# A three-branch block and two hybrid layers on one core: HGRN-2 traced among RWKV-7's steps, x normalized before the products, the gates last

## The chip, the cores and the metric

The kernel runs on one core of one Trainium2 chip. The metric is device microseconds (us) of a whole execution. Three runs of the kernel before gave 3648.86, 3641.06 and 3642.4 us, a median of 3642.4 us. Engines are named as in the profile: PE is TensorE (PEld its weight loads), DVE VectorE, ACT ScalarE, POOL GpSimd, SP SyncE, which here only starts transfers.

## The reference, cut to what matters

512 tokens of 1024 features pass through a first block and then two hybrid layers (the change touches only the first block and how its neighbours are traced). The first block in float32:

```
xn = rmsnorm(x, norm1_w);  p = xn @ w_in            # z, xbc, dt | rwkv | hgrn | gates
y_ssm  = ssd_branch(z, xbc, dt)   @ w_branch_ssm    # state space, chunks of 128 tokens
y_rwkv = rwkv7_branch(p_rwkv)     @ w_branch_rwkv   # 8 heads of 64, both directions
y_hgrn = hgrn2_branch(p_hgrn)     @ w_branch_hgrn   # 4 heads of 128, both directions
gates  = sigmoid(p_gate)                            # 3 x 1024 columns
x = x + (g0 * y_ssm + g1 * y_rwkv + g2 * y_hgrn) @ w_out
x = x + ffn(rmsnorm(x, norm2_w))

# RWKV-7, per head and direction:
S_t = S_{t-1} diag(w_t) + (S_{t-1} (-kk_t)) (kk_t * a_t)^T + v_t k_t^T ;  y_t = S_t r_t
# HGRN-2, per head and direction:
S_t = diag(f_t) S_{t-1} + k_t v_t^T ;  o_t = S_t^T q_t
```

## The kernel before, in words

Activations lie with features on the partitions, 512 tokens along the free axis, split into two float16 parts (`xh`, `xl`). Weights come from DRAM in units of 512 KB (eight 128 x 128 blocks), each split into a high and a low float16 part (`_emit_unit`, ACT and DVE, in the first block every second background unit ACT and POOL, line 1055). A product of 128 output features is 8 blocks x 3 matmuls of 512 columns (`fm_g`, lines 1169 to 1171); a product by token (`tm`) is 96 matmuls of 128 columns. I call the first kind a wide product, of 24 wide matmuls.

A scheduler orders the instructions of each engine. Work traced as foreground keeps its order roughly; work traced as background (`bgmode`), after it, is moved into the gaps. Foreground wide products in the first block all go to one PSUM bank (`acc=1`), background ones to two other banks (`bg`). Each kind has a weight stream of its own, in the order of the tables FOREGROUND and BACKGROUND.

The first block runs so. `start()` loads x, splits x times the gain into parts, sums squares, and leaves 1/rms as a row `rb` (line 1297), by which every product is multiplied when it leaves PSUM (`conv_pad` line 247, HGRN line 801, gates line 1310). Then `rwkv()` goes through four tiles of two heads. For each tile `rwkv_mid` builds the causal products `G` of the 8 chunks x 2 heads x 2 directions and inverts I + A: the 32 x 32 diagonal blocks go out to DRAM (`pd`, line 432) and come back as `M` with one block's rows per partition (line 441); DVE solves for X in two interleaved chains of small operations (lines 463 and 466); X goes out to DRAM (line 470) and back into `G` (line 473); the blocks above the diagonal come from small matmuls (lines 480 to 491). `rwkv_scan` then steps through 8 chunks with both directions side by side, and inside it `rwkv_in` prepares the next tile. I call the part of a tile from the first exchange to the scan the inverse.

HGRN-2 (`hgrn`, four heads; per head three wide products and two by token, then seven levels of masked score products, lines 840 to 848) and 16 of the 24 gate tiles are traced after `rwkv` as background. SSD comes next as foreground, with background of its own: the up projections of the RWKV and HGRN outputs (`wbr`, `wbh`), the last 8 gate tiles, and the up projection of SSD's output (`wbs`). The up projections sum into `mg` (line 1333); the output projection `wo1` and the feed-forward follow, then the two hybrid layers.

Of the kernel before, what the change touches and what calls it, by code (L numbers as in the profile page):

```python
# [12 lines left out]
BF16 = mybir.dt.bfloat16  # L13
AF = mybir.ActivationFunctionType
# [5 lines left out]
T = 512  # L20
# [12 lines left out]
def blocks(*ws):  # L33
    """[K, N] matrices with N a multiple of 128 -> units of 8 blocks of 128 x 128, each
    unit with its rows on the partitions; the blocks run over columns, then rows."""
    seq = []
    for w in ws:
        k, n = w.shape
        seq.append(w.reshape(k // 128, 128, n // 128, 128).transpose(2, 0, 1, 3).reshape(-1, 128, 128))
    b = np.concatenate(seq) if len(seq) > 1 else seq[0]  # L40
    return np.ascontiguousarray(b.reshape(-1, UB, 128, 128).transpose(0, 2, 1, 3))


def paired(a, b):
    """Blocks of two matrices, a column tile of each in turn."""
# [25 lines left out]
def gate_up(a, name, *ws):  # L71
    """The column tiles FF7 for products in sevens, the others for plain ones."""
# [5 lines left out]
def odd_even(w):  # L78
    """The odd and the even column tiles."""
# [5 lines left out]
#: Column tiles of the second block's w_in (without the 16 mLSTM gates) in the order of use.  # L85
# [9 lines left out]
#: The same for the first block's (without the 32 steps of the state space branch).  # L95
# [8 lines left out]
def first_constants():  # L104
    """Selectors of heads and masks of the chunks' orders."""
# [16 lines left out]
class Packed:  # L122
    """Small vectors side by side in one array; the program finds them by name."""
# [46 lines left out]
def arrange(x):  # L170
    """The kernel's inputs as the program reads them."""
# [55 lines left out]
def run(gen):  # L227
    """A generator's work at once; its result."""
# [6 lines left out]
class First:  # L235
    """The first block's layer: state space (SSD), RWKV-7 and HGRN-2 branches."""
# [4 lines left out]
    def conv_pad(self, ps, side):  # L241
        """psum / rms with zeros on either side."""
# [4 lines left out]
        nc.vector.tensor_tensor(out=xp[:, 2:T + 2], in0=ps, in1=self.rb, op=ALU.mult)  # L247
        return xp

# [1 line left out]
    def shifted(self, it, n, out):  # L251
        """Token shift in both directions of column tile n."""
# [6 lines left out]
    def half_sigmoid(self, out, ps, hb):  # L259
        """0.5 + 0.5 tanh: the sigmoid of (psum / WS + bias), hb half the bias."""  # L260
# [14 lines left out]
    def rwkv(self, yd):  # L275
        """Chunks of 64 tokens, both directions side by side, a tile of two heads after the
        other; the backward direction keeps its keys and values reversed within the chunks."""
# [34 lines left out]
        for j in range(4):  # L312
            self.rwkv_mid(j)
            scan = self.rwkv_scan(j)
            for c in range(8):
                if c == 2 and j < 3:
                    run(self.rwkv_in(j + 1, it, lx))
                if c == 4 and j < 3:
                    self.rwkv_decays(j + 1, lx)
                next(scan)  # L320
            run(scan)
            self.rwkv_out(j, gx, yd)

    def rwkv_in(self, j, it, lx):
        """What a tile of two heads needs of the projections."""
# [7 lines left out]
        yield from self.shifted(it, j, r)  # L333
        ks = self.bank()
# [5 lines left out]
        yield from self.shifted(it, 8 + j, vf)  # L340
        pr = self.bank()
# [54 lines left out]
    def rwkv_mid(self, j):  # L396
        """Keys and queries with their decays, all causal products of a chunk, (I + A)^-1."""
# [17 lines left out]
        # (source: b or k, i) x (target: kk or r, t) for every direction, chunk and head  # L415
# [12 lines left out]
        # the 32 x 32 diagonal blocks of I + A inverted, one block's even or odd rows a partition  # L428
        pd = self.t(self.dram, [2, 32, 32, 32], "pd")
# [1718 lines left out]
```

## Time and profile before

| what | us |
|---|---|
| runs: median (lowest, highest) | 3642.4 (3641.06, 3648.86) |
| profiled execution: its span | 3644.9 |
| start: loads, norm, first products | 0 to 87.4 |
| RWKV-7 with HGRN-2 and gates behind it | 87.4 to 680.0 |
| SSD up to its last matmul | 680.0 to 960.5 |
| rest of the background up to `wo1` | 960.5 to 1034.8 |
| `wo1`, feed-forward, two hybrid layers | 1034.8 to 3644.9 |

The table cuts the span at places that can be found in the trace: 87.4 and the starts of the later tiles (228.2, 380.6, 519.9) are the first causal products of a tile on PE (line 424's), 680.0 the end of the last tile's output, 960.5 the end of SSD's last small matmul (line 767), 1034.8 the first matmul of `wo1`. The profiled execution's span is 0.07% above the median of the runs.

### The profile page before, as it was taken

The numbers are of one execution on the slowest core, as the hardware profiler recorded it, in microseconds if no ns is written. First come the engines' busy times: TensorE is split into PE (matmuls) and PEld (weight loads), VectorE is DVE, ScalarE is ACT, GpSimd is POOL, SyncE is SP. The second block draws the span as 40 slices with busy tenths as digits, with TensorE's granted clock in tenths as the row PEclk, the third lists the DMA queues.
The fourth block names the chain that finished last, engine by engine and source line by source line (L and its number), as shares of the span: only waits on it lengthen the run. The fifth ranks groups of instructions, "written<-read, shape, count | busy, mean of one in ns | idle before, by whom it ended". The sixth has DMA issues, their size and how long they took to land. (4 is left out here: it accounts for less than half of the span.)

```text
span 3644.9 us, 60827 instructions
## 1 busy us (share of the span) xinstructions
PE 3388.2 (93%) x23758; PEld 2045.0 (56%) x23758; DVE 2751.5 (75%) x5599; ACT 1624.4 (45%) x3033; POOL 751.7 (21%) x762
## 2 busy tenths in 40 slices
PE   7899898898899999999989999999999989999998
PEld 3566565554445567655545545568655545545567
DVE  6767867587577798688767677788688767767788
ACT  4232232455444444364456544444364456634344
POOL 1322223223332212101110131211101120132211
PEclk9897999999999999999999999999999999999999
DMA  4211212333352234322323353335322323353233
GB/s 137 70 49 40 64 40 63 131 111 113 106 171 94 97 99 142 108 74 75 106 76 100 106 170 99 98 112 159 106 73 72 105 81 101 108 172 123 94 99 98
DMA packets 151157, 368.17 MB, mean 101 GB/s; under 512 B 44098, under 2 KB 47428, under 8 KB 150868
## 3 DMA queue, kind: packets, MB, share of 16 engines
q1 hardware_dynamic: 117492, 336.03, 29.5%
q0 software_dynamic: 7680, 23.00, 1.9%
q10 hardware_dynamic: 25696, 5.25, 0.8%
q8 instruction: 186, 3.05, 0.3%
q14 instruction: 103, 0.84, 0.1%
HBM read 322.72 MB, written 40.04 MB: 100 GB/s over the span
## 5 line engine op out<-in xcount | busy, mean ns | idle before, releaser
L1169 PE MATMUL acc<-xh,whi 128*128 128x512 f16 x1224 | 469.3, 383 | 33.0 <-DVE w L753 11.8
L1171 PE MATMUL acc<-xh,wlo 128*128 128x512 f16 x1224 | 469.1, 383 | 20.6 <-DVE wlo L1059 20.3
L1170 PE MATMUL acc<-xl,whi 128*128 128x512 f16 x1224 | 469.6, 384 | 0.0
L1058 ACT ACTIVATE whi<-wst 128x1024 f16<-128x1024 f32 x240 | 250.0, 1049 | 263.4 <-PE acc L1170 141.7
L1059 DVE SCALAR_TENSOR_TENSOR wlo<-wst,whi 128x1024 f16<-128x1024 f32 x240 | 319.0, 1329 | 15.4 <-ACT whi L1058 14.9
L1169 PE MATMUL bg<-xh,bhi 128*128 128x512 f16 x788 | 311.1, 395 | 9.9 <-DVE hi L811 8.2
L1171 PE MATMUL bg<-xh,blo 128*128 128x512 f16 x788 | 310.5, 394 | 5.8 <-DVE reset L309 3.2
L1170 PE MATMUL bg<-xl,bhi 128*128 128x512 f16 x788 | 311.1, 395 | 0.0
L1171 PEld LDWEIGHTS <-wlo 128*128 128x128 f16 x1632 | 160.7, 98 | 232.5 <-DVE wlo L1059 46.4
L1170 PEld LDWEIGHTS <-whi 128*128 128x128 f16 x1632 | 160.5, 98 | 213.0 <-issue 41.6
L1169 PEld LDWEIGHTS <-whi 128*128 128x128 f16 x1632 | 161.1, 99 | 193.8 <-ACT whi L1058 13.5
L1428 POOL TENSOR_TENSOR w<-w,w 128x512 f32<-128x512 f32 x66 | 117.0, 1773 | 445.4 <-DVE w L1428 280.1
L1059 DVE SCALAR_TENSOR_TENSOR blo<-bst,bhi 128x1024 f16<-128x1024 f32 (+1 forms) x156 | 180.5, 1162 | 34.4 <-ACT bhi L1058 32.7
L1204 PE MATMUL acc<-whi,xh 128*128 128x128 f16 x1152 | 195.1, 219 | 2.1 <-DVE bias L1843 1.2
L1058 ACT ACTIVATE bhi<-bst 128x1024 f16<-128x1024 f32 (+1 forms) x156 | 136.4, 887 | 133.0 <-PE bg L1170 95.7
L1206 PE MATMUL acc<-whi,xl 128*128 128x128 f16 x1152 | 195.0, 219 | 0.0
L1205 PE MATMUL acc<-wlo,xh 128*128 128x128 f16 x1152 | 195.0, 219 | 0.0
L1171 PEld LDWEIGHTS <-blo 128*128 128x128 f16 x1172 | 117.0, 100 | 131.3 <-issue 16.3
L1170 PEld LDWEIGHTS <-bhi 128*128 128x128 f16 x1172 | 117.1, 100 | 130.7 <-issue 29.0
L1169 PEld LDWEIGHTS <-bhi 128*128 128x128 f16 x1172 | 117.3, 100 | 114.7 <-issue 15.1
L1204 PEld LDWEIGHTS <-xh 128*128 128x128 f16 x1408 | 139.9, 99 | 15.2 <-issue 5.0
L1205 PEld LDWEIGHTS <-xh 128*128 128x128 f16 x1408 | 140.0, 99 | 6.8 <-issue 5.0
(665 smaller groups left out, 9117.2 us busy)
## 6 DMA issues: line engine op xcount, KB each, us to landing
wst<-win SPq DMA_DIRECT2D x92, 512.0 KB, 3.6
bst<-win SPq DMA_DIRECT2D x64, 512.0 KB, 3.7
wst<-wff SPq DMA_DIRECT2D x60, 512.0 KB, 3.6
bst<-w SPq DMA_DIRECT2D x44, 512.0 KB, 3.5
gd<-bw SPq DMA_DIRECT2D x88, 256.0 KB, 2.1
ug<-gd SPq DMA_DIRECT2D x88, 256.0 KB, 2.7
wst<-w SPq DMA_DIRECT2D x34, 512.0 KB, 3.5
wst<-wf SPq DMA_DIRECT2D x30, 512.0 KB, 3.4
```

The source lines that it names most:

```text
L1058: nc.scalar.activation(out=hi[:, h], in_=st[:, h], func=AF.Copy, scale=WS)
L1059: nc.vector.scalar_tensor_tensor(out=lo[:, h], in0=st[:, h], scalar=WS, in1=hi[:, h], op0=ALU.mult, op1=ALU.subtract)
L1169: mm(ps, lhsT=wh, rhs=h[:, k, :], start=(k == 0), stop=False)
L1170: mm(ps, lhsT=wh, rhs=l[:, k, :], start=False, stop=False)
L1171: mm(ps, lhsT=wl, rhs=h[:, k, :], start=False, stop=(k == nk - 1))
L1204: mm(o, lhsT=xh, rhs=wh, start=(k == 0), stop=False)
L1205: mm(o, lhsT=xh, rhs=wl, start=False, stop=False)
L1206: mm(o, lhsT=xl, rhs=wh, start=False, stop=(k == 7))
L1428: tt = lambda eng, o, x, y, op=ALU.add: eng.tensor_tensor(out=o, in0=x, in1=y, op=op)
```

## The change

Five things are changed together; comments and docstrings are also taken out, so line numbers shift by about 15. First, `start()` sums squares first and multiplies x by `rb` before the split, so that products need no factor by token: what multiplied on DVE or POOL becomes an ACT copy or an ACT tanh out of PSUM. Second, HGRN's level mask is a predicated copy in place of a multiplication and an addition. Third, the exchange of the 32 x 32 blocks goes through PE and PSUM in place of DRAM, the solve is one chain, and `M` and `X` are read at a stride of 32 floats. Fourth, the scan's state is added by PE (a product with the identity). Fifth, `hgrn` is a generator that yields after each part, and `beside()` takes 0.62 of a step at each step of `rwkv`; its weights stand in FOREGROUND among RWKV's, its products go to the one foreground bank, and all 24 gate tiles are traced in SSD's background, ahead of the up projections.

```
 conv_pad:
-        nc.vector.tensor_tensor(out=xp[:, 2:T + 2], in0=ps, in1=self.rb, op=ALU.mult)
+        nc.scalar.activation(out=xp[:, 2:T + 2], in_=ps, func=AF.Copy, scale=IWS)
 rwkv:
         for j in range(4):
-            self.rwkv_mid(j)
+            for _ in self.rwkv_mid(j):
+                beside()
...
                 next(scan)
+                beside()
 rwkv_mid, exchange and solve:
-        for q in range(2):
-            s = slice(32 * q, 32 * q + 32)
-            nc.scalar.dma_start(out=pd[q].rearrange("m i t -> i m t"), in_=G[s, :, s])
...
-            (nc.scalar, nc.sync)[q].dma_start(out=M[s], in_=pd.rearrange("q m i t -> (q m) i t"))
...
+        M = self.t(mid, [128, 1024], "M")
+        for u in range(2):
+            ps = self.b("S")
+            for t in range(16):
+                for q in range(2):
+                    s = slice(32 * q, 32 * q + 32)
+                    mm(ps[s, 32 * t:32 * t + 32], lhsT=G[:, :, 32 * q + 16 * u + t], rhs=self.ident[:, s], start=True, stop=True)
+            for h in range(2):
+                nc.scalar.copy(out=M[64 * h:64 * h + 64, 512 * u:512 * u + 512], in_=ps[0:64])
+        Mv = M.rearrange("p (t i) -> p i t", i=32)
...
+        Xv = X[:, 0:1024].rearrange("p (t r) -> p r t", r=32)
...
         for i in range(31):
-            for c, n in rs:    # c: two chains
-                v.tensor_tensor(out=t, in0=X[c][:, 0:n, i:i + 1]..., in1=M[:, i:i + 1, ts]..., op=ALU.mult)
-            for c, n in rs:
-                v.tensor_tensor(out=X[c][:, 0:n, ts], in0=X[c][:, 0:n, ts], in1=t, op=ALU.subtract)
+            v.tensor_tensor(out=t, in0=Xv[:, rs, i:i + 1]..., in1=Mv[:, i:i + 1, ts]..., op=ALU.mult)
+            v.tensor_tensor(out=Xv[:, rs, ts], in0=Xv[:, rs, ts], in1=t, op=ALU.subtract)
+            if i % 6 == 5:
+                yield
-        for q in range(2):
-            for c in range(2):
-                nc.scalar.dma_start(out=pd2[:, :, :, c, q]..., in_=X[c][64 * q:64 * q + 64])
-        for q in range(2):
-            nc.scalar.dma_start(out=G[s, :, s], in_=pd2[q].rearrange("m r c e t -> (r c e) m t"))
+        for k in range(8):
+            for h in range(2):
+                mm(px[:, 64 * k:64 * k + 64], lhsT=X[:, o:o + 128], rhs=self.ident[:, 64 * h:64 * h + 64], start=(h == 0), stop=(h == 1))
...
+                if q:
+                    nc.scalar.copy(out=dst, in_=src)
+                else:
+                    v.tensor_copy(out=dst, in_=src)
+        for i in range(32):
+            mm(pt[i // 16][0:32, ...], lhsT=Xv[:, i // 2 * 2 + 1], rhs=self.ident[...], start=True, stop=True)
 rwkv_scan, the state:
-                    v.tensor_tensor(out=zf, in0=z.rearrange("p d k -> p (d k)"), in1=pz[:, 0:256], op=ALU.add)
-                    v.tensor_tensor(out=four_v(zf), in0=four_v(zf), in1=zb, op=ALU.mult)
+                    if z is not None:
+                        mm(o, lhsT=self.ident, rhs=z[:, d], start=True, stop=False)
...
+                v.tensor_tensor(out=zn..., in0=pz[:, 0:256]..., in1=zb, op=ALU.mult)
 hgrn, the level mask:
-                    v.tensor_tensor(out=t, in0=po..., in1=hm[:, l:l + 1].to_broadcast([128, 4, 128]), op=ALU.mult)
-                    nc.gpsimd.tensor_tensor(out=sc, in0=sc, in1=t, op=ALU.add)
+                    v.copy_predicated(sc, hm[:, l:l + 1].bitcast(U16).to_broadcast([128, 4, 128]), po...)
 first:
+                def beside():
+                    at[0] += 0.62
+                    while at[0] >= 1:
+                        at[0] -= 1
+                        next(hg, None)
-                self.rwkv(yd[0])
+                self.rwkv(yd[0], beside)
...
                     self.background(
+                        self.gates("w1", 14, 24, gd),
                         self.up(gd, 1, "wbr", *yr, 4, True),
                         self.up(gd, 2, "wbh", *yg, 4),
-                        self.gates("w1", 14, 8, gd),
                         self.up(gd, 0, "wbs", *ysm, 8, False, rbs),
 start:
             for k in range(8):
-                self.norm_tile(k, x[:, k], gain)
-            self.norm_end()
+                self.square_sums(k, x[:, k], None, eng=nc.vector)
+            self.norm_end(1.0)
+            for k in range(8):
+                (nc.gpsimd if k % 3 == 1 else nc.vector).tensor_tensor(out=x[:, k], in0=x[:, k], in1=self.rb, op=ALU.mult)
+                self.split(self.xh[:, k, :], self.xl[:, k, :], x[:, k], self.col(gain, k))
 gates, in the first block:
-                nc.scalar.copy(out=g, in_=ps)
-                nc.gpsimd.tensor_tensor(out=g, in0=g, in1=self.rb, op=ALU.mult)
+                nc.scalar.activation(out=g, in_=ps, func=AF.Tanh, scale=0.5 * IWS)
-FOREGROUND = [ ("w1", 0, 14), ("w1", 38, 58), ...
+FOREGROUND = [ ("w1", 0, 5), ("w1", 58, 63), ("w1", 5, 8), ("w1", 63, 68), ...
-    nc = _bacc.Bacc("TRN2", target_bir_lowering=False, num_devices=1)
+    nc = _bacc.Bacc("TRN2", target_bir_lowering=False, num_devices=1, dynamic_dma_scratch_size=4096)
```

How the order of instructions changes is shown at three places. The first is ACT's queue at the end of the first tile's inverse. Before (`bw` is a gate, `hw` HGRN's, `w` the transposed blocks):

```order
L1309 COPY bw_4320<-bg_4287 128x512
L1313 ACTIVATE bw_4320<-bw_4320 128x512
L815 ACTIVATE hw_4087<-hg_3981 128x512
L470 DMA pd_121_712<-X_114_562 512x1x32 x2
L470 DMA pd_121_712<-X_113_561 512x1x32 x2
L473 DMA G_506<-pd_121_712 32x32x32 x2
L482 COPY w_736<-S_719 32x512
```

Now the same place, with HGRN's products (`hk`, `hi`, `hg`) leaving PSUM between the two exchanges:

```order
L445 COPY M_648<-S_649 64x512 x2
L445 COPY M_648<-S_684 64x512 x2
L1074 ACTIVATE whi_818<-wst_816 128x1024
L821 ACTIVATE hk_612<-acc_757 128x512
L826 ACTIVATE hi_815<-acc_822 128x512
L1074 ACTIVATE whi_947<-wst_945 128x1024
L830 ACTIVATE hg_944<-acc_951 128x512
L1074 ACTIVATE whi_1312<-wst_1310 128x1024
L489 COPY G_514<-T_1052 32x8x32
L494 COPY M_648<-S_1053 32x16x32
```

The DMAs are gone from ACT's queue; copies out of PSUM stand in their place, behind HGRN's evacuations.

The second place is DVE in the middle of the first tile's solve. Before, the two chains (`tx_111` with `X_113`, `tx_112` with `X_114`) alternate:

```order
L466 TENSOR_TENSOR X_113_561<-X_113_561,tx_111_559 128x2x27
L466 TENSOR_TENSOR X_114_562<-X_114_562,tx_112_560 128x2x25
L463 TENSOR_TENSOR tx_111_559<-X_113_561,M_558 128x52
L463 TENSOR_TENSOR tx_112_560<-X_114_562,M_558 128x48
L466 TENSOR_TENSOR X_113_561<-X_113_561,tx_111_559 128x2x26
L466 TENSOR_TENSOR X_114_562<-X_114_562,tx_112_560 128x2x24
```

Now, one chain, with HGRN's work and a weight split among it:

```order
L471 TENSOR_TENSOR tx_719<-X_720,M_648 128x126
L472 TENSOR_TENSOR X_720<-X_720,tx_719 128x6x21
L1075 SCALAR_TENSOR_TENSOR wlo_819<-wst_816,whi_818 128x1024
L822 TENSOR_SCALAR hp_611<-hk_612,hc_107_542,hc_106_541 128x512
L471 TENSOR_TENSOR tx_719<-X_720,M_648 128x120
L823 TENSOR_SCALAR hk_612<-hp_611 128x512
L472 TENSOR_TENSOR X_720<-X_720,tx_719 128x6x20
```

Each operation of the chain now reads what the one ahead of it wrote.

The third place is POOL at SSD's end. Before, the up projections' sums (`mg`) stand among SSD's last steps (`sy`, `sqa`):

```order
L763 TENSOR_TENSOR w_8013<-sy_7928 128x512
L686 DMA crow_8256<-crd_6647 128x1024
L764 TENSOR_TENSOR sqa_6853<-sqa_6853,w_8013 128x512
L1333 TENSOR_TENSOR mg_6464<-mg_6464,ug_8696 128x512
L1333 TENSOR_TENSOR mg_6464<-mg_6464,ug_8713 128x512
L750 TENSOR_TENSOR sy_8122<-sy_8122,sec_8141 128x384
```

Now SSD's last `sqa` is followed by the first `mg`:

```order
L766 TENSOR_TENSOR sy_7712<-sy_7712,sec_7753 128x384
L777 TENSOR_TENSOR w_7795<-sy_7712 128x512
L778 TENSOR_TENSOR sqa_6263<-sqa_6263,w_7795 128x512
L1242 TENSOR_TENSOR ssq_7803<-ssq_7803,mhalf 128x4
L1071 TENSOR_TENSOR blo_8618<-bst_8615,bhi_8617 128x1024
L1071 TENSOR_TENSOR blo_8691<-bst_8688,bhi_8690 128x1024
L1071 TENSOR_TENSOR blo_8770<-bst_8767,bhi_8769 128x1024
L1071 TENSOR_TENSOR blo_8849<-bst_8846,bhi_8848 128x1024
L1348 TENSOR_TENSOR mg_5874<-mg_5874,ug_8843 128x512
```

All sums into `mg`, from the HGRN output's on, now come after SSD's end. On PE, the wide matmuls behind SSD's last small matmul and ahead of `wo1` go from 313 to 428 in the order; in the RWKV stage, first block's start included, wide matmuls go from 798 (235 foreground, 563 background) to 701 (520 and 181), in SSD from 780 to 752. Behind `wo1` PE's order is the same.

## Rows read from the trace of the kernel before

**Rows 1.** First line of the page: the profiled span.

```profile
span 3644.9 us, 60827 instructions
```

**Rows 2.** Busy time by stage (first line: columns; x counts instructions).

```profile
core 0: us, PE busy (x) PEld busy (x) DVE busy (x) ACT busy (x) POOL busy (x), PEclk, DMA share, GB/s
0.00:87.40 87.40, 64.25 (x317) 31.39 (x317) 59.03 (x101) 41.65 (x64) 15.80 (x33) 0.98 0.45 143
87.40:680.00 592.60, 533.17 (x4114) 359.96 (x4115) 425.83 (x1175) 172.11 (x374) 169.36 (x143) 0.90 0.20 55
680.00:960.50 280.50, 254.12 (x1505) 140.67 (x1504) 216.16 (x358) 147.12 (x294) 86.63 (x93) 0.97 0.38 122
960.50:1034.80 74.30, 71.31 (x324) 32.64 (x324) 31.57 (x40) 28.20 (x41) 30.72 (x20) 0.96 0.40 132
1034.80:3644.90 2610.10, 2465.36 (x17505) 1480.37 (x17503) 2018.87 (x3927) 1235.30 (x2260) 449.14 (x473) 0.99 0.34 107
```

**Rows 3.** The same by RWKV tile, then the third tile's products, inverse, scan.

```profile
228.20:380.60 152.40, 141.38 (x1057) 97.90 (x1056) 107.23 (x304) 42.18 (x92) 36.00 (x37) 0.85 0.16 42
519.90:680.00 160.10, 137.65 (x1048) 92.38 (x1048) 102.25 (x298) 44.51 (x95) 50.49 (x33) 0.87 0.21 60
380.60:393.50 12.90, 12.39 (x85) 9.24 (x85) 10.61 (x38) 0.63 (x1) 3.30 (x2) 1.00 0.00 1
393.50:467.60 74.10, 63.83 (x565) 40.85 (x563) 65.48 (x186) 21.85 (x34) 25.67 (x23) 0.91 0.33 90
467.60:519.90 52.30, 52.20 (x386) 36.54 (x385) 35.97 (x79) 21.86 (x62) 13.26 (x11) 1.00 0.10 31
```

**Rows 4.** Timeline, third tile's exchanges: start, duration, engine, line, operation.

```profile
396.87 0.93 ACTq L432 DMA_DIRECT2D pd<-G  x2
407.67 0.28 DVE L463 TENSOR_TENSOR tx<-X,M 128x31 f32<-128x31 f32 x2
438.19 3.79 ACTq L470 DMA_DIRECT2D pd<-X  x4
453.71 0.64 PE L480 MATMUL S<-ident,G 32*32 32x32 f32 x16
```

**Rows 5.** Timeline of DVE in the first tile: two dependent operations; two chains.

```profile
104.30 0.74 DVE L256 SCALAR_TENSOR_TENSOR fr<-xp,cols,fr 128x512 f32<-128x512 f32 x1
105.07 0.75 DVE L257 SCALAR_TENSOR_TENSOR fr<-xp,cols,fr 128x512 f32<-128x512 f32 x1
...
118.86 0.33 DVE L463 TENSOR_TENSOR tx<-X,M 128x54 f32<-128x54 f32 x2
119.10 0.33 DVE L466 TENSOR_TENSOR X<-X,tx 128x54 f32<-128x54 f32 x2
```

**Rows 6.** Groups by line, 25 to 1035 us: busy, mean ns, idle before.

```profile
L848 POOL TENSOR_TENSOR hs<-hs,hw 128x512 f32<-128x512 f32 x20 | 36.0, 1800 | 73.4 <-DVE hw L847 48.6 <-DVE X L466 24.8
L1310 POOL TENSOR_TENSOR bw<-bw,rb 128x512 f32<-128x512 f32 x24 | 33.9, 1414 | 72.4 <-ACT bw L1309 72.4
L840 DVE TENSOR_TENSOR hw<-hk,hr 128x512 f32<-128x512 f32 x28 | 28.6, 1020 | 2.0 <-PE H L856 1.9
L247 DVE TENSOR_TENSOR xp<-acc,rb 128x512 f32<-128x512 f32 x26 | 17.9, 687 | 20.3 <-PE acc L1171 20.2
```

**Rows 7.** Timeline of PE: wide matmuls at full and at half clock.

```profile
450.48 0.63 PE L1171 MATMUL bg<-xh,blo 128*128 128x512 f16 x1
450.91 0.50 PE L1169 MATMUL bg<-xh,bhi 128*128 128x512 f16 x1
...
929.24 0.38 PE L1169 MATMUL bg<-xh,bhi 128*128 128x512 f16 x1
929.45 0.38 PE L1170 MATMUL bg<-xl,bhi 128*128 128x512 f16 x1
```

**Rows 8.** Timeline of DVE in a later layer: a strided read.

```profile
1816.60 1.05 DVE L1623 TENSOR_TENSOR w<-acc,rb 128x512 f32<-128x512 f32 x1 [1.43 <-PE acc L1171]
```

**Rows 9.** Timeline of DVE in the start: 1/rms as a row.

```profile
31.41 0.69 DVE L1297 COPY rb<-T 128x512 f32<-128x512 f32 x1 [3.04 <-PE T L1296]
```

More of the change, by code (lines that the diff above doesn't have):

```diff
@@ L13 @@
 BF16 = mybir.dt.bfloat16
+U16 = mybir.dt.uint16
 AF = mybir.ActivationFunctionType
@@ L273, in lora, with rwkv @@
         return ps
-    def rwkv(self, yd):
+    def rwkv(self, yd, beside):
         nc, v = self.nc, self.nc.vector
@@ L316, in rwkv @@
                 if c == 2 and j < 3:
-                    run(self.rwkv_in(j + 1, it, lx))
+                    for _ in self.rwkv_in(j + 1, it, lx):
+                        beside()
                 if c == 4 and j < 3:
@@ L320, in rwkv @@
                 next(scan)
+                beside()
             run(scan)
@@ L458, in rwkv_mid @@
         for i in range(31):
-            ts, nt = slice(i + 1, 32), 31 - i
-            rs = [(c, (i - 2 * c) // 4 + 1) for c in range(2) if i >= 2 * c]
-            for c, n in rs:
-                t = tx[c][:, 0:n * nt].rearrange("p (a b) -> p a b", b=nt)
-                v.tensor_tensor(out=t, in0=X[c][:, 0:n, i:i + 1].to_broadcast([128, n, nt]), in1=M[:, i:i + 1, ts].to_broadcast([128, n, nt]), op=ALU.mult)
-            for c, n in rs:
-                t = tx[c][:, 0:n * nt].rearrange("p (a b) -> p a b", b=nt)
-                v.tensor_tensor(out=X[c][:, 0:n, ts], in0=X[c][:, 0:n, ts], in1=t, op=ALU.subtract)
@@ L467, in rwkv_mid @@
-        pd2 = self.t(self.dram, [2, 32, 8, 2, 2, 32], "pd2")
-        for q in range(2):
-            for c in range(2):
-                nc.scalar.dma_start(out=pd2[:, :, :, c, q].rearrange("q m r t -> (q m) r t"), in_=X[c][64 * q:64 * q + 64])
-        for q in range(2):
-            s = slice(32 * q, 32 * q + 32)
-            nc.scalar.dma_start(out=G[s, :, s], in_=pd2[q].rearrange("m r c e t -> (r c e) m t"))
+            n, nt, rs, ts = i // 2 + 1, 31 - i, slice(1, i // 2 * 2 + 2, 2), slice(i + 1, 32)
@@ new lines, in rwkv_mid @@
+            t = tx[:, 0:n * nt].rearrange("p (a b) -> p a b", b=nt)
+            v.tensor_tensor(out=t, in0=Xv[:, rs, i:i + 1].to_broadcast([128, n, nt]), in1=Mv[:, i:i + 1, ts].to_broadcast([128, n, nt]), op=ALU.mult)
+            v.tensor_tensor(out=Xv[:, rs, ts], in0=Xv[:, rs, ts], in1=t, op=ALU.subtract)
+            if i % 6 == 5:
+                yield
+        px, pt = self.b("T"), [self.b("S") for _ in range(2)]
+        for k in range(8):
+            for h in range(2):
+                o = 128 * k + 1 - h
+                mm(px[:, 64 * k:64 * k + 64], lhsT=X[:, o:o + 128], rhs=self.ident[:, 64 * h:64 * h + 64], start=(h == 0), stop=(h == 1))
@@ new lines, in rwkv_mid @@
+        st = M[0:32].rearrange("p (m i) -> p i m", i=32)
+        for k in range(4):
+            p = slice(32 * k, 32 * k + 32)
+            for q in range(2):
+                s = slice(32 * q, 32 * q + 32)
+                src = px[p].rearrange("p (k q m) -> p q k m", k=8, q=2)[:, q]
+                dst = G[s, :, s].rearrange("p m (k t) -> p t k m", t=4)[:, k]
+                if q:
+                    nc.scalar.copy(out=dst, in_=src)
+                else:
+                    v.tensor_copy(out=dst, in_=src)
@@ L475, in rwkv_mid @@
+        for i in range(32):
+            mm(pt[i // 16][0:32, 32 * (i % 16):32 * (i % 16) + 32], lhsT=Xv[:, i // 2 * 2 + 1], rhs=self.ident[:, 64 * (i % 2):64 * (i % 2) + 32], start=True, stop=True)
+        nc.scalar.copy(out=st[:, 0:16], in_=pt[0][0:32].rearrange("p (i m) -> p i m", m=32))
+        v.tensor_copy(out=st[:, 16:32], in_=pt[1][0:32].rearrange("p (i m) -> p i m", m=32))
+        st = M[0:32].rearrange("p (m i) -> p m i", i=32)
         lo, hi = slice(0, 32), slice(32, 64)
@@ L479, in rwkv_mid @@
             for n, m in enumerate(ms):
-                nc.tensor.transpose(px[lo, 32 * n:32 * n + 32], G[lo, m, lo], self.ident[lo, lo])
-            st = self.w()
-            nc.scalar.copy(out=st[lo], in_=px[lo])
-            px = self.b("S")
-            for n, m in enumerate(ms):
-                mm(px[hi, 32 * n:32 * n + 32], lhsT=G[lo, m, hi], rhs=st[lo, 32 * n:32 * n + 32], start=True, stop=True)
+                mm(px[hi, 32 * n:32 * n + 32], lhsT=G[lo, m, hi], rhs=st[:, m], start=True, stop=True)
             xt = self.w()
@@ L526, in rwkv_scan @@
                 mm(pu[lo, q], lhsT=G[lo, mi(d, e), 0:64], rhs=wn[lo, q], start=True, stop=True)
-            v.tensor_copy(out=uv[0][lo, chs[0]], in_=pu[lo, 0:128])
-            nc.scalar.copy(out=uv[1][lo, chs[1]], in_=pu[lo, 128:256])
+            nc.scalar.copy(out=uv[0][lo, chs[0]], in_=pu[lo, 0:128])
+            v.tensor_copy(out=uv[1][lo, chs[1]], in_=pu[lo, 128:256])
             if not last:
@@ L631, in ssd @@
         for i in range(4):
-            v.scalar_tensor_tensor(out=da[:, i], in0=pd[:, 32 * i:32 * i + 32], scalar=self.rt[:, i:i + 1], in1=self.row("dtb"), op0=ALU.mult, op1=ALU.add)
+            v.scalar_tensor_tensor(out=da[:, i], in0=pd[:, 32 * i:32 * i + 32], scalar=IWS, in1=self.row("dtb"), op0=ALU.mult, op1=ALU.add)
         v.tensor_scalar(out=fl(da), in0=fl(da), scalar1=-1.0, scalar2=None, op0=ALU.mult)
```

85 lines of the change are left out of this document (38 added, 47 removed), and 23 rows, old and new, of tables (BACKGROUND, FOREGROUND).

## The prediction

> **What bounds the kernel now.** I read the busy time by stage first. The last stage is 2610 of 3644.9 us with PE busy 2465 of them [rows 1, 2]; the change leaves PE's order there as it is, so it counts as nothing unless a transfer gets slower. What can move is the first 1035 us, where PE is busy 923 us and yet short of work: at full clock a wide matmul follows the one before it by 0.21 us, though its own record is 0.38, at half clock by 0.43 [rows 7]. Busy PE is therefore no measure of need. Counting every matmul of the first 1035 us at the closest spacing its kind shows at full clock gives 811 us; the same count over the new order gives 843. So 224 us of the 1035 are loss, and the change adds 32 us of PE work (identity products of the scan's state and of the exchanges); it can only win by cutting the loss.
>
> Where the loss sits: the RWKV stage has the lowest clock, 0.90, and a DMA share of only 0.20 [rows 2]. The second and fourth tile stand out with 152 and 160 us at 0.85 and 0.87 [rows 3]; the third, in full: 12.9 us of causal products, 74.1 of inverse at clock 0.91, 52.3 of scan at 1.00 with PE busy all through [rows 3]. So the scan is PE-bound, and the inverse is not: DVE is busy 65.5 of its 74.1 us. The timeline of the inverse [rows 4] shows three waits in a row. The blocks leave for DRAM at 396.87, the solve starts at 407.67 (10.8 us), X leaves at 438.19 (30.5 us), and the first product on what came back is at 453.71 (15.5 us).
>
> **The exchanges.** The way out and back costs 10.8 + 15.5 = 26.3 us per tile. What replaces it: 64 small matmuls for M, and 16 such take 0.64 us [rows 4], so 2.6, with four copies of 512 elements of about 0.69 (the evacuation at line 247) [rows 6], half of them beside the matmuls: 5 us. Back: 16 + 32 small matmuls and ten short copies on two engines: 7 us. The 32 transposes and a copy behind them go too: of the 13.9 us from 453.71 to the stretch's end at 467.6 I keep 8. Both ends: if the copies queue on ACT behind HGRN's evacuations as the order shows, each exchange may wait two or three evacuations, 2 us; DMA waits at least 0.
>
> **The solve.** Before, 120 operations in two chains; now 62 in one. From the two chains, a pair of operations starts every 0.24 us [rows 5], so 120 take 15 us. In one chain each waits for the end of the last: 104.30 + 0.74 leads to 105.07, 0.03 late. One operation's length: 0.74 at 512 elements [rows 5], and 0.33 - 0.12 = 0.21 at 54, hence 0.15 + 0.00116 per element. The 62 handle 5712 elements: 62 x 0.18 + 6.6 = 18 us. But M and X are now read and written at a stride of 32 floats. The nearest row is a strided read of 512 elements at 1.05 [rows 8] beside 0.69 for the plain one [rows 6]: 1.67 times per element, so 11 in place of 6.6 and 22 us in all. Bounds 18 and 22 (and 27, if writes pay as well); I take 22, the nearest row being a strided one. The other 15 us of DVE in the solve's 30.5 shrink to 7, as HGRN's operations in the inverse fall from 27 to 10 by the order. The solve: 22 + 7 = 29 us, almost no gain.
>
> [...]
>
> **HGRN in the foreground.** Its 20 products move from the two background banks to the one foreground bank, and 56 of the inverse's 130 wide matmuls leave it; the scan of the third tile has 124 in place of 64. 60 x 0.216 = 13 us, and the state's products with the identity another 2 to 3: the scan grows from 52.3 to 68. HGRN's DVE work, which goes there too, is hidden, since DVE is busy 36.0 of 52.3 [rows 3]: 53 of 68. If the cover goes, the scan becomes DVE-bound at a few us more. A new wait stands there: a foreground product must wait until ACT has emptied the one bank, 0.17 for the last matmul's end and some 0.69 for the copy; what is queued behind it on PE are the scan's small matmuls, and DVE waits for those.
>
> **The tile and the stage.** 12.9 + (3.4 + 5 + 29 + 7 + 8 = 52) + 68 = 133 us in place of 139.3. That is a small gain for the third tile; but the others were 141, 152 and 160 because their clock was lower [rows 3], and with the DRAM waits gone I expect them to look like the third. Four times 133 is 532 in place of 592.6: -61 us.
>
> **The start.** The products now wait for the norm. Before, the row of 1/rms was there at 31.41 [rows 9] while background products, which needed only the split, ran well ahead of it; now nothing runs until the row is there, by my estimate at about 25, since eight splits of 0.75 on DVE no longer stand among the sums; then a tile of x takes 1.4 us (0.69 multiplied, 0.75 split) and a product of eight tiles 11 us. The chain that RWKV hangs on loses almost nothing, PE loses background work: +5 (0 to 10).
>
> **SSD and what follows it.** SSD loses 28 wide matmuls (780 to 752) on a PE that isn't full: -4 (-6 to 0). Behind SSD's last matmul 115 more must be done, 428 in place of 313: 115 x 0.216 = 24.8, at that stretch's clock of 0.96 +27 us. It is the other side of moving the gates last: the sums into `mg` all come after SSD's end.
>
> **At nothing.** The additions at 848 and the multiplications at 1310 took POOL 36 and 34 us [rows 6], POOL being busy 169 of 592.6 [rows 2]: hidden; should POOL's absence shorten DVE operations (line 840 has a mean of 1.02 us where others of that size take 0.74), up to 28 x 0.28 = 8 us come on top. The predicated copy isn't in the trace: 0.69 to 1.05 by the two rows named, times 20, against about 0.69 before, so 0 to +7 us on DVE, and I take 0; below 0 only if reading two inputs from three places is cheaper than a multiplication, for which there is no reason. The evacuations that go from DVE to ACT (26 of 0.69) are hidden, ACT being busy 172 of 592.6. For the smaller descriptor ring no row tells anything; nothing is taken, and 1% of the last stage would be 26 us.
>
> **The sum.** +5 - 61 - 4 + 27 = -33 us on 3644.9, so 3612 in the profiled execution's terms; it lies 0.07% above the median, which makes 3610.
>
> **The rivals.** (a) The loss is mostly the half clock and it goes entirely. For it: the clock of 0.85 and 0.87 just where the tiles are long [rows 3]. Then the stage comes near 500 us, its counted need being 445: +5 - 93 - 4 + 27 = -65, 3577. Against it: the inverse has fewer wide matmuls to fill its holes than before.
>
> (b) Slower: the one foreground bank. 34 products (20 of HGRN and 14 of RWKV) wait for an evacuation, 0.17 + 0.69 and two hops, about 1 us each, and the 181 background matmuls left (563 before) can't fill the holes: 34 us; with the solve at 27 in place of 22 (20 us over four tiles) the stage stays at 532 + 34 + 20 = 586. The sum is +5 - 7 - 4 + 27 = +21, 3664. For it: PE was full in the scan only thanks to the background [rows 3], and HGRN's heads now share every in-order queue with RWKV's chain. Against it: SSD runs with one foreground bank at a clock of 0.97 [rows 2]. It decides from a stage of 565 + 7 = 572 us on.
>
> (c) No change: the stage at 557 to 572 us, the tail eats the gain, 3642.
>
> (d) The change doesn't do what it says: the steps of HGRN do not fall into RWKV's waits, as 0.62 of a step at each of some 88 calls puts most in the scan, which was PE-bound already. Then the scan grows by 16 and the inverse gives 22 back: this is what the sum has for the third tile, and the other tiles gain no more than it, 4 x 6 = 24 us; the stage is 568 and the time as in (c).
>
> **Chances.** The forecast has 0.45, (a) 0.23, (c) with (d) 0.12, (b) 0.20. A change under 0.2%, 7.3 us, can't be told from none by the runs shown. So faster 0.67, the same 0.11, slower 0.22 (b, and the slow half of c). The likeliest case's own range is 3590 to 3630; to hold 8 in 10 it reaches to 3560, past (a) by a little as an evacuation on ACT and an undisturbed DVE may give more, and to 3658, most of the way to (b).
>
> **What would show it.** Right: no transfers of `pd`; the three waits of the inverse together under 45 us where they were 56.8; the solve's operations 0.3 us apart or more; the RWKV stage at 520 to 545 us with a clock above 0.93; from SSD's last small matmul to `wo1` about 100 us; the last stage at 2610 within 5. Wrong: a stage over 565 with PE waiting for ACT to empty `acc`; a predicated copy over 1.05 us; a last stage that is longer, with transfers landing later than before.

## The result and the profile after

The changed kernel takes 3691.9 us (median of 4 runs, 3688.9 to 3702.8) where the kernel before takes 3645.6: a ratio of 1.0132, 95% interval 1.0111 to 1.0153. It is 46 us slower; 3610 was forecast and the range ended at 3658. The profiled execution is the slowest of the four, 3702.8 us with a span of 3701.1.

The busy time by stage, cut at the same places of the program (columns as in [rows 2]):

```profile
core 0: us, PE busy (x) PEld busy (x) DVE busy (x) ACT busy (x) POOL busy (x), PEclk, DMA share, GB/s
0.00:90.80 90.80, 63.33 (x277) 30.01 (x277) 57.76 (x94) 44.19 (x69) 19.38 (x33) 1.00 0.46 146
90.80:229.90 139.10, 131.75 (x1214) 97.33 (x1214) 98.67 (x201) 44.60 (x93) 18.04 (x21) 0.94 0.11 37
229.90:402.00 172.10, 161.75 (x1252) 116.15 (x1251) 107.77 (x230) 49.77 (x108) 26.97 (x27) 0.81 0.11 38
402.00:561.90 159.90, 152.58 (x1257) 112.70 (x1256) 106.03 (x227) 49.49 (x108) 25.76 (x23) 0.87 0.12 41
561.90:699.60 137.70, 127.78 (x1175) 98.42 (x1175) 86.39 (x217) 38.17 (x88) 19.66 (x16) 0.91 0.11 35
699.60:980.90 281.30, 254.76 (x1513) 143.42 (x1512) 195.54 (x330) 153.39 (x317) 68.97 (x81) 0.97 0.34 113
980.90:1081.70 100.80, 96.67 (x436) 43.47 (x435) 48.11 (x60) 30.51 (x41) 40.44 (x25) 0.97 0.50 155
1081.70:3701.10 2619.40, 2469.37 (x17505) 1480.42 (x17503) 2019.42 (x3927) 1234.44 (x2260) 451.56 (x473) 0.99 0.34 107
```

Against [rows 2]: the start is +3.4 us, the RWKV stage 608.8 in place of 592.6 (+16; forecast -61), SSD the same, the stretch behind it 100.8 in place of 74.3 (+26.5; forecast +27), the last stage +9. The DMA share of the RWKV stage fell from 0.20 to 0.11, so the DRAM exchanges are gone, and yet no time came of it. (The profiled execution is the slowest, so these differences add up to 56 us and not to 46.) What the reader is to see: PE is busy 94% of these four tiles, DVE falls from 426 to 399 us, and the second tile, which had the lowest clock already [rows 3], is 172 us at a clock of 0.81 in place of 152 at 0.85.

The new groups of instructions on PE, and the two that carry the solve and the mask (busy, mean ns, idle before):

```profile
L480 PE MATMUL T<-ident,X 128*128 128x64 f32 x128 | 21.3, 298 | 15.0 <-DVE X L472 15.0
L554 PE MATMUL S<-z,ident 128*128 128x128 f32 x96 | 24.9, 347 | 0.0
L443 PE MATMUL S<-ident,G 128*32 128x32 f32 x512 | 15.5, 222 | 0.5 <-DVE G L434 0.5
L493 PE MATMUL S<-ident,X 128*32 128x32 f32 x256 | 15.3, 221 | 0.0
L472 DVE TENSOR_TENSOR X<-X,tx 128x126 f32<-128x126 f32 (+22 forms) x124 | 40.4, 326 | 3.5
L471 DVE TENSOR_TENSOR tx<-X,M 128x126 f32<-128x126 f32 (+22 forms) x124 | 38.9, 314 | 13.9 <-ACT M L445 10.6
L862 DVE COPY_PREDICATED hs<-hgm,H 128x512 f32<-128x512 uint16 x20 | 14.5, 725 | 10.3 <-PE H L861 10.2
```

The exchange is 21.3 + 15.5 + 15.3 = 52 us of PE (lines 480, 443, 493; the transposes that they replace, line 480 of the kernel before, took 5), the state's products 25. I had the exchange at 2.6 us a tile for M and a share of 7 for X, and the state's products at 2 to 3 a tile. The X chain is (40.4 + 38.9) / 4 = 20 us a tile as forecast (22), the masked copy 0.73 us.

### The profile page after: what moved, and what is told of

Read it like the earlier page. It is cut to its first block, busy times and chain, and to the rows that moved or that the text cites. A ratio compares the mean times of both kernels' runs of the same rounds, so it can differ in the third digit from the quotient of the medians.

```text
span 3701.1 us, 62065 instructions
## 1 busy us (share of the span) xinstructions
PE 3458.0 (93%) x24622; PEld 2121.9 (57%) x24622; DVE 2719.7 (73%) x5282; ACT 1644.6 (44%) x3083; POOL 670.8 (18%) x699
## 5 line engine op out<-in xcount | busy, mean ns | idle before, releaser
L1185 PE MATMUL acc<-xh,whi 128*128 128x512 f16 x1320 | 509.3, 386 | 37.2 <-DVE w L770 8.1
L1187 PE MATMUL acc<-xh,wlo 128*128 128x512 f16 x1320 | 508.8, 385 | 20.6 <-DVE wlo L1075 20.5
L1186 PE MATMUL acc<-xl,whi 128*128 128x512 f16 x1320 | 508.4, 385 | 1.7 <-DVE xl L1239 1.7
L1074 ACT ACTIVATE whi<-wst 128x1024 f16<-128x1024 f32 x260 | 271.2, 1050 | 329.2 <-PE acc L1186 213.1
L1187 PE MATMUL bg<-xh,blo 128*128 128x512 f16 x692 | 271.0, 392 | 0.5 <-DVE blo L1075 0.5
L1186 PE MATMUL bg<-xl,bhi 128*128 128x512 f16 x692 | 271.0, 392 | 0.0
L1185 PE MATMUL bg<-xh,bhi 128*128 128x512 f16 x692 | 270.9, 392 | 0.0
L1220 PE MATMUL acc<-whi,xh 128*128 128x128 f16 x1408 | 248.1, 223 | 1.6 <-DVE bias L1861 1.0
L1222 PE MATMUL acc<-whi,xl 128*128 128x128 f16 x1408 | 247.8, 223 | 0.0
L1221 PE MATMUL acc<-wlo,xh 128*128 128x128 f16 x1408 | 247.7, 223 | 0.0
```

Of the source, the lines that this page charges most:

```text
L1074: nc.scalar.activation(out=hi[:, h], in_=st[:, h], func=AF.Copy, scale=WS)
L1185: mm(ps, lhsT=wh, rhs=h[:, k, :], start=(k == 0), stop=False)
L1186: mm(ps, lhsT=wh, rhs=l[:, k, :], start=False, stop=False)
L1187: mm(ps, lhsT=wl, rhs=h[:, k, :], start=False, stop=(k == nk - 1))
L1220: mm(o, lhsT=xh, rhs=wh, start=(k == 0), stop=False)
L1221: mm(o, lhsT=xh, rhs=wl, start=False, stop=False)
```

## The experiments

Sixteen runs followed, each beside the kernel before on its chip; `after_again` is the changed kernel once more, with two executions. Times are medians; the ratio is against the kernel before, with its interval. Differences below are between medians; where the chips differ I give the one by the ratios too. All of these kernels keep the smaller descriptor ring of the change; no run undoes it.

| kernel | parts of the change in it | us | before, same chip | ratio (95%) |
|---|---|---|---|---|
| changed kernel | 1 2 3 4 5 | 3691.9 | 3645.6 | 1.0132 (1.0111, 1.0153) |
| dram_exch | 1 2 4 5 | 3606.1 | 3641.7 | 0.9898 (0.9884, 0.9912) |
| dve_state | 1 2 3 5 | 3647.5 | 3641.7 | 1.0017 (1.0005, 1.0030) |
| hgrn_bg | 1 2 3 4 | 3672.2 | 3641.7 | 1.0087 (1.0073, 1.0100) |
| gates_early | all, 16 gates earlier | 3686.0 | 3641.7 | 1.0124 (1.0106, 1.0143) |
| dram_dve | 1 2 5 | 3606.6 | 3640.8 | 0.9897 (0.9882, 0.9912) |
| dram_dve_hbg | 1 2 | 3666.5 | 3640.8 | 1.0066 (1.0050, 1.0082) |
| m_pe_x_dram | 1 2 4 5, M of 3 | 3630.6 | 3640.8 | 0.9967 (0.9954, 0.9980) |
| dummy_pe | 1 2 4 5, unread matmuls | 3646.5 | 3640.8 | 1.0017 (1.0007, 1.0028) |
| x_pe_m_dram | 1 2 4 5, X of 3 | 3615.5 | 3642.4 | 0.9931 (0.9918, 0.9943) |
| no_mask | 1 5 | 3628.5 | 3642.4 | 0.9965 (0.9955, 0.9975) |
| norm_back | 2 5 | 3609.3 | 3642.4 | 0.9917 (0.9903, 0.9930) |
| hgrn_fg_only | 5 | 3629.3 | 3642.4 | 0.9967 (0.9954, 0.9979) |
| after_again | all, second profile | 3709.6 | 3646.6 | 1.0173 (1.0147, 1.0200) |
| after_warm | all, added matmuls | 3681.7 | 3646.6 | 1.0095 (1.0082, 1.0107) |
| dram_warm | 1 2 4 5, added matmuls | 3624.4 | 3646.6 | 0.9945 (0.9932, 0.9957) |
| x_pe_dve | 1 2 5, X of 3 | 3624.7 | 3646.6 | 0.9943 (0.9927, 0.9958) |

**One part undone.** My theory after the result was that HGRN's fixed place in the scans had lengthened them (theory 1); the rivals were PE's added work (theory 2) and the gates' place (theory 3).

```
hgrn_bg:     -  self.rwkv(yd[0], beside)          + self.rwkv(yd[0], lambda: None); hgrn and 16 gates as background
gates_early: +  for g in range(4): run(self.gates("w1", 22 + 4 * g, 4, gd, 8 + 4 * g))   # behind hgrn, background
dram_exch:   -  mm(ps[s, ...], lhsT=G[...], rhs=self.ident[:, s])   + nc.scalar.dma_start(out=pd[q]..., in_=G[s, :, s]); two chains
dve_state:   -  mm(o, lhsT=self.ident, rhs=z[:, d])   + v.tensor_tensor(out=zf, in0=z..., in1=pz..., op=ALU.add)
```

> The changed kernel with its fifth part undone: HGRN traced after RWKV as background, whole heads alternating with 16 gate tiles, the weight tables as before; normalized x, masked copies, PE exchanges and PE state stay. Theory 1 (HGRN's products and scores, put into the scans in a fixed order, lengthen them: 90 us over four scans): the scans return to 54 to 64 us each, the stage behind SSD to 74 us, time about 3610 to 3630. Theory 2 (the PE work of the exchanges and the state is what costs): only the stage behind SSD returns, -27 us against the changed kernel, about 3665.

> The changed kernel with only the place of 16 gate tiles undone: they are traced as background right behind HGRN, the up projections of RWKV and HGRN ahead of the last 8 gates; HGRN stays in the foreground. Theory 3 (the gates traced last are the loss: PE has holes in the RWKV stage that only gates could fill): the stretch behind SSD falls from 101 to about 74 us and nothing else grows, 3665. Against it (PE is full in the RWKV stage, as its 94 % busy says): what leaves the end comes back as a longer RWKV stage, 3685 to 3695.

> The changed kernel with its third part undone: 32 x 32 blocks through DRAM, two chains, contiguous M and X. Theory 2 (PE work of the exchanges, some 60 us of small matmuls on a PE that is full): the RWKV stage falls by 20 to 40 us, time 3655 to 3670. Theory 1: the DRAM waits of 26 us a tile come back where HGRN in the foreground can't fill them, +15 to +40 us, 3705 to 3730.

> The changed kernel with the addition of the scan's state back on DVE, the 96 identity matmuls (48 pairs) gone from PE. Theory 2: 18 us of PE records go, stage -10 to -20, time 3672 to 3682. Theory 1: one more DVE operation in each scan step's chain against 0.4 us less on PE, no change within 5 us.

Theory 1 was right on the scans and wrong on the time: without HGRN in the foreground they take 54, 48, 60 and 48 us and the RWKV stage 508, but the time is 3672, since HGRN then ends at 698 us, after RWKV at 604, and holds SSD up. Theory 3 fell: the gates' place is worth 6 us, which the two intervals don't tell from nothing; what left the end came back in SSD (306 us in place of 281). Theory 2 had the right side, and both of its times were far too high (3655 to 3670 and 3672 to 3682): the third part of the change (the exchange, with its solve in one strided chain) is worth 86 us, the state 44. The stages with the exchange through DRAM:

```profile
92.50:658.20 565.70, 535.67 (x4303) 371.74 (x4304) 372.50 (x1098) 177.65 (x397) 95.83 (x100) 0.93 0.21 58
658.20:919.40 261.20, 237.76 (x1442) 134.24 (x1441) 192.64 (x325) 146.62 (x300) 67.27 (x80) 0.98 0.37 118
919.40:994.40 75.00, 72.70 (x333) 32.77 (x332) 40.33 (x51) 22.02 (x31) 34.09 (x22) 0.98 0.48 153
```

All three stages fall, the stretch behind SSD too, though the gates are traced as late as in the changed kernel: the work that left PE in the RWKV stage made room there for background work, and the two later stages have 71 and 103 PE records fewer. `wo1` starts at 994.4 in place of 1081.7, 87 us. About 47 of these are the exchange's own matmuls less those it replaces. For the rest see the clock: added up from the trace, the stage of 608.8 us holds 152 us at a granted clock of 0.50 (the rest is at 1.00), that of 565.7 holds 80. If all work takes twice as long there, as the wide matmuls do (0.43 us from one to the next in place of 0.21 [rows 7]), half of the difference, 36 us, is lost by it (an estimate).

**Work or waiting.**

```
dummy_pe:     dram_exch +  mm(ps[s, ...], lhsT=G[:, :, 32 * q + 16 * u + t], rhs=self.ident[:, s])   # 64, 16 and 32 a tile, unread
m_pe_x_dram:  dram_exch +  M by matmuls and four ACT copies; X through DRAM
x_pe_m_dram:  changed   +  nc.scalar.dma_start(out=pd[q]..., in_=G[s, :, s])   # M through DRAM, X through PE
x_pe_dve:     x_pe_m_dram with dve_state
```

> The kernel with the exchange through DRAM (3606 us) and, beside it, matmuls of the PE exchange's shapes and number whose results nobody reads: 64 on G, 16 and 32 on X a tile. Theory A (PE is the bound of the first 1035 us, so added matmuls cost their own 55 us and more by a lower granted clock): 3650 to 3690. Theory B (the PE exchange cost its time by its chain: copies out of PSUM behind HGRN's, the strided solve): 3606 to 3620.

> M through PE and four copies (read at a stride of 32 floats), X contiguous, in two chains, back through DRAM. Theory A: M's matmuls were 15 us of the exchange's 55 on PE, so a fifth to a third of its 86 us: 3620 to 3640; and 10 us less of waiting at each M that only counts if PE has nothing else. Theory B: no more than 10 from 3606 either way.

> The complement of the run with M through PE: M out and back through DRAM (contiguous), X in one strided chain, back through PE. X's matmuls are 39 of the 55 us that the exchange puts on PE. If the cost follows PE's matmuls, this is 40 to 65 above the kernel with both through DRAM (3606): 3646 to 3671, and M's part was 24, so that the two add up to about 86. If it were the waits of the longest exchange, M through DRAM would make it no better than the changed kernel, 3685 to 3695.

> M through DRAM, X through PE, the state added on DVE. With PE's state it was 3615. If PE's matmuls cost what they last: 18 us of state products less, 3597 to 3603. If the state costs nothing while one exchange goes through DRAM (as with both through DRAM): 3610 to 3620.

Matmuls that nobody reads cost 40 us (43 by the ratios): PE's work by itself accounts for nearly half of the 86, with all the DRAM waits still there. M through PE costs 24, X through PE 9 (25 and 12 by the ratios; both with PE's state); my 40 to 65 for X was a miss, and the parts don't add up: 33 against 86. x_pe_dve has a ratio of 0.9943 against 0.9931, outside both of its forecasts, so taking the state's products off PE gives nothing back beside one exchange.

What is missing is the clock. Every execution on record has its mean granted clock; (1 - clock) x span is then the time lost if everything at half clock takes twice as long (an estimate; medians over the executions, the changed kernel's two runs together):

| kernel | executions | granted clock | lost, us | time without it |
|---|---|---|---|---|
| dram_exch | 5 | 0.977 | 83 | 3527 |
| M through PE | 5 | 0.978 | 80 | 3550 |
| X through PE | 5 | 0.983 | 61 | 3554 |
| dummy_pe | 11 | 0.982 | 66 | 3579 |
| dve_state | 11 | 0.977 | 84 | 3562 |
| changed kernel | 6 | 0.966 | 124 | 3575 |

Without the clock's share the parts do add up: M costs 23 us, X 27, both 48, and the unread matmuls 52. Of the 86 us about 50 are PE's work, and the rest is that the changed kernel loses some 40 us more by its clock than dram_exch. Of the state's 44 only 13 are left. (Counting a loss of 0.4 in place of half, an estimate from the two stretches of the same matmuls below, 61.6 us at 0.50 and 40.9 at 0.87, gives M 22, X 24, both 59, the unread ones 50, the state 23.)

**The clock.** The second profile of the changed kernel, and two kernels with six matmuls of 256 columns more in each scan step but the last:

```
after_warm, dram_warm:
+  for k in range(6):
+      mm(pt[:, 256:512], lhsT=self.xh[:, k, 0:128], rhs=self.xh[:, k, 0:256], start=True, stop=True)   # unread
```

> The changed kernel once more, for a second profile. In the first the granted clock of the RWKV stage was 0.87, with 152 us of it at half clock and one stretch of 62 us; the other kernels with HGRN in the foreground had 42 to 107 us. If the half clock belongs to this kernel: 110 to 160 us again, in long stretches in the scans. If it was that execution's: 40 to 80, and a time near 3660.

> The changed kernel with six more wide matmuls of 256 columns in every scan step but the last, whose results nobody reads: 28 x 6 x 0.108 = 18 us of PE work. Theory H (the clock falls in scans that hold almost no wide float16 matmul, and that is half of the loss): the half clock of the stage falls by 60 us or more, the time by 5 to 30 in spite of the added work, 3660 to 3687. Otherwise: +15 to +25, 3707 to 3717.

> The same six matmuls in the kernel with the exchange through DRAM (3606), whose scans have more wide matmuls and a clock of 0.93. Under theory H little to win: +5 to +18; as a control for the price of the added work.

The changed kernel's second profile has the same tiles, cut at its own first products, the last three to a tenth of a microsecond:

```profile
91.30:227.60 136.30, 128.69 (x1215) 95.02 (x1215) 98.58 (x201) 44.62 (x94) 18.04 (x21) 0.96 0.12 38
227.60:399.70 172.10, 161.73 (x1253) 116.10 (x1252) 107.77 (x230) 49.76 (x108) 26.99 (x27) 0.81 0.11 38
399.70:559.60 159.90, 152.57 (x1258) 112.69 (x1257) 106.02 (x227) 49.49 (x108) 25.73 (x23) 0.87 0.12 41
559.60:697.30 137.70, 127.78 (x1175) 98.43 (x1175) 86.38 (x218) 38.16 (x88) 19.66 (x16) 0.91 0.11 35
360.00:422.00 62.00, 60.02 (x253) 45.35 (x254) 26.31 (x73) 11.55 (x36) 8.81 (x7) 0.51 0.03 9
```

The last line is one stretch at half clock, from the second tile's scan into the third tile; in the first profile it lies at 363 to 424 us, again 61 long. PE is busy 60 of the 62 us and leaves 253 records (a float32 matmul leaves two: 512 at line 443 for the 256 on G). What they are, in the first profile's timeline:

```profile
386.06 1.11 PE L886 MATMUL H<-ident,hr 128*128 128x128 f32 x4
387.10 1.11 PE L545 MATMUL S<-w,G 64*64 64x64 f32 x8
388.15 0.79 PE L554 MATMUL S<-z,ident 128*128 128x128 f32 x2
388.73 0.63 PE L1185 MATMUL bg<-xh,bhi 128*128 128x512 f16 x1
389.16 0.64 PE L893 MATMUL H<-hi,hw 128*128 128x128 f32 x2
```

Float32 matmuls of the scan and HGRN, and few wide ones between: the background is held for later, and the stage has 675 wide matmuls, with the exchange through DRAM 817. With the added matmuls the stage, and 64 us at that place, look so:

```profile
91.10:666.60 575.50, 543.11 (x5022) 398.69 (x5023) 390.43 (x870) 178.71 (x394) 87.31 (x86) 0.95 0.11 38
360.00:424.00 64.00, 61.54 (x477) 42.42 (x477) 41.37 (x113) 17.08 (x41) 7.90 (x7) 0.89 0.08 26
```

Clock 0.95 in place of 0.87 to 0.88, the stage 31 to 33 us shorter with an estimated 18 us more to do (168 matmuls at half the 0.21 us of a wide one [rows 7]); the ratio is 0.8% below after_again's and 0.4% below the first comparison's. In the kernel with the exchange through DRAM the same matmuls cost 0.5%, 17 us, their own price.

That dense wide work lifts the clock is not shown by this. gates_early has the same matmuls as the changed kernel in the same order: all 5171 records up to the end of the RWKV stage agree in names and shapes. The first line is the long stretch in the changed kernel's first profile, the second the same records in gates_early, the third its whole stage, the last the stage with unread small float32 matmuls:

```profile
363.20:424.80 61.60, 60.45 (x255) 45.56 (x256) 25.91 (x73) 10.75 (x35) 8.42 (x8) 0.50 0.03 9
365.00:405.90 40.90, 38.12 (x255) 29.14 (x256) 24.38 (x71) 10.52 (x34) 6.41 (x6) 0.87 0.05 14
92.20:684.40 592.20, 553.14 (x4895) 405.52 (x4896) 398.80 (x872) 182.02 (x397) 90.44 (x87) 0.91 0.12 39
90.90:677.50 586.60, 560.59 (x5132) 403.07 (x5133) 373.46 (x1093) 172.35 (x389) 93.99 (x99) 0.96 0.18 52
```

The same matmuls took 40.9 us there in place of 61.6, with nothing added, so PE's order alone doesn't decide on that stretch. dummy_pe's clock is 0.96 where dram_exch has 0.93, so added small float32 work went with a higher clock as well. And theory H had its count wrong: the changed kernel's scans hold 99, 127, 124 and 30 wide matmuls, those of dram_exch 46, 42, 80 and 24. What holds is that all five executions with the added matmuls have a granted clock of 0.976 to 0.979, all six of the changed kernel 0.961 to 0.971. So by the estimate some 40 us of the changed kernel's loss are half clock; why its clock is the lower one stays open.

**The other parts.**

```
dram_dve:      dram_exch and dve_state                  dram_dve_hbg: the same and hgrn_bg
no_mask:       dram_dve -  v.copy_predicated(sc, ...)    + v.tensor_tensor(mult), nc.gpsimd.tensor_tensor(add)
norm_back:     dram_dve -  x * rb before the split       + products times rb as before
hgrn_fg_only:  no_mask and norm_back
```

> Both the exchange through DRAM and the state's addition on DVE: parts 1, 2 and 5 of the change alone. Theory A: the state's matmuls on PE (18 us and clock) cost 44 us in the changed kernel; here at a granted clock that is already higher, 15 to 40: 3566 to 3591. Theory B: within 5 us of 3606.

> As the one before, with HGRN and 16 gates in the background again: parts 1 and 2 of the change alone, beside the kernel before. If HGRN in the foreground is worth what it was meant to be, this is slower than the one with it by 10 to 40 us, near 3605 to 3630; if the foreground order costs, it is faster. Against the kernel before, x normalized first and the masked copies: my sum had +5 for the start and nothing else, so 3640 to 3647.

> Parts 1 and 5 of the change (x normalized first, HGRN in the foreground, gates last), the mask again a DVE multiplication and a POOL addition, exchange and state as before. My sum had the masked copy at nothing: 3606 within 7. If POOL's additions stretch DVE's operations or the scores' chain hangs on them: 3612 to 3625.

> Parts 2 and 5: the mask as a predicated copy, HGRN in the foreground, gates last; x split first and scaled by 1/rms after the products, as before. Parts 1 and 2 together cost 26 us beside the kernel before when HGRN was in the background. If part 1 costs it (products wait for the norm, PE idle 17 us more in the first 40): 3580 to 3600. If foreground products are helped by evacuations without DVE: 3606 to 3630.

> Part 5 alone on the kernel before: HGRN stepped in the foreground among RWKV's steps, the gates last. With parts 1 and 2 it was worth 60 us (3666 to 3606). If its worth doesn't hang on them: about 3581, the fastest of all. If it needs the evacuations on ACT and the POOL free: 3606 to 3640.

HGRN in the foreground with the gates last is worth 60 us beside parts 1 and 2 (3666.5 to 3606.6) and 13 alone (3642.4 to 3629.3); by the estimate from the granted clock some 23 of the 60 and nothing of the 13 are left without the clock's share. The masked copy is worth 20 us where HGRN is in the foreground (3629.3 to 3609.3; 3628.5 to 3606.6): I had put it at nothing. Why is not shown: in no_mask's profile nothing waits for POOL's addition; what the trace does show is that the operations of line 850 on DVE take 0.99 us with it and 0.74 without. x normalized first is worth nothing there, within 3 us. Parts 1 and 2 without 5 are 26 us slower than the kernel before, where my sum had 3640 to 3647; the profile shows a RWKV stage of 560 us at a clock of 0.85 and an SSD stage of 330, as HGRN ends at 699 us; which of the two parts does it was not tried. The fastest kernels are dram_dve and dram_exch, 1.0% below the kernel before: the change without its exchange through PE. norm_back, at 0.8%, is hardly told from them.

## Why the prediction was wrong

**The failed step is "The exchanges".** With the third part of the change undone, the kernel takes 3606 us in place of 3692, and the miss is gone; the solve in one strided chain is not it, since x_pe_m_dram has that and takes 3615. The step priced 64 matmuls for M by a row of 32 x 32 transposes (0.64 us for 16), X's 48 by the like 1.9 more, 4.5 us of PE a tile; they measured 52 / 4 = 13. The form differs: G and X are taken over all 128 partitions, X in blocks of 128 x 64, and each of these float32 matmuls leaves two records where a transpose leaves one (line 480: 128 records now for 64 matmuls on X, 128 before for 128 transposes). The step also counted them only as latency: my first paragraph has 32 us of added PE work, and the sum has no term for it. As latency it was right. In the third tile the solve starts 5.1 us behind the first matmul for M (forecast 5), lasts 29.9 (29), and the first product on what comes back follows 7.2 us later (7). But PE had no time to spare: dummy_pe shows what that work costs when it brings nothing, 40 us, some 52 without the clock's share.

**"The tile and the stage" failed with it.** The inverse did get shorter: in the first tile from 85 us (first product to scan) to 65. But I expected the second and fourth tile to recover the third's clock "with the DRAM waits gone". The clock fell from 0.90 to 0.87. The DRAM waits had not been the cause: the kernel that keeps them, dram_exch, has 0.93. The scans grew from 56, 66, 55 and 54 us to 75, 99, 84 and 57 where I had 68 (from the first product of line 526, now 545, to the next tile; the last to its last product). The third scan holds 124 wide matmuls as forecast and still takes 84: 17 us of it are at half clock. Over the stage the half clock costs an estimated 76 us, where a clock above 0.93 would have left at most 37; that is about half of the 77 by which the stage missed.

**The rival (b) had the right side and the wrong mechanism.** It held that the one foreground bank would cost. PE's idle time in the stage fell to 35 us from 59, and HGRN in that bank is worth 60. Rival (a) fell with the clock. Rival (d) is half borne out: HGRN's products do go into the scans and not into the waits (wide matmuls of the four scans: 68, 51, 64 and 56 before, 99, 127, 124 and 30 now, but 46, 42, 80 and 24 in dram_exch, which has more of them in the inverse), and the first three scans grew by 19 to 33 us, where it had 16.

**What held.** Besides the exchanges' latency, the start (+3.4; I had +5), the stretch behind SSD (100.8; I had 101), the solve (20 us of operations; 22), and the price of strided operands: 135 elements at a time take 0.43 us from one start to the next, my formula gives 0.15 + 0.03 + 135 x 0.00194 = 0.44, without the stride 0.34:

```profile
267.26 0.40 DVE L471 TENSOR_TENSOR tx<-X,M 128x135 f32<-128x135 f32 x1
267.69 0.40 DVE L472 TENSOR_TENSOR X<-X,tx 128x135 f32<-128x135 f32 x1
268.13 0.38 DVE L471 TENSOR_TENSOR tx<-X,M 128x126 f32<-128x126 f32 x1
```

That dram_exch comes out at 3606 where I had 3610 for all five parts is luck: it includes 20 us of the masked copy that I had at nothing, and none of the exchange on which my sum was built.

**At nothing** was wrong for the masked copy, 20 us. The last stage's +9 us (2619 in this profile, 2616 in the second) lies within 2607 to 2620 of the other kernels, whose code there is the same; I take it as scatter; a cost of the smaller descriptor ring isn't seen in it.

## What to carry to other kernels

Here PE was busy 90% of the stage [rows 2], and 64 of the 74 us of the inverse with its waits on transfers [rows 3]: other work ran under them. Replacing such a transfer by work on the very engine that is short of time has to be priced at that engine's rate, by a row of the same shape, and against the whole budget of the stages that share background work. A shorter latency, forecast to the microsecond, was worth nothing here. A dummy of the added work, unread, is the cheapest way to tell work from waiting. When the effects of parts don't add up, look at the granted clock of every execution before looking for a mechanism: here they add up once its share is taken out. And before an order of instructions is blamed for a clock, look for another kernel with the same order.

## What the runs showed of the hardware

A stretch of 62 us at a granted clock of 0.51 came back at the same place of the program in a second execution, while PE was busy 97% of it, mostly with small float32 matmuls; the same matmuls in the same order took 40.9 us in gates_early, at a clock of 0.87 in place of 0.50. With an estimated 18 us of added wide float16 matmuls the changed kernel's stage took 575.5 us in place of 606.0 and 608.8, at a clock of 0.95 in place of 0.87 to 0.88; small float32 matmuls added to dram_exch went with 0.96 in place of 0.93. What makes the clock fall is not known. A float32 matmul that takes 128 x 32 of G costs 15.5 / 256 = 0.06 us of PE, and one that takes 128 x 64 of X 21.3 / 64 = 0.33 by busy time; PE idles another 15 us in all before the latter, waiting for the chain on DVE. Float32 matmuls leave two records each (512 for the 256 on G), the transposes of the kernel before one (128 for 128). A predicated copy of 128 x 512 float32 out of PSUM took 0.73 us.
